# RMS norm rows by one product with ones and a logarithm-exponential pair, and the third norm's steps written among the output projection's blocks

## The chip, the cores and the metric

The kernel runs on one core of a Trainium2 chip. The metric is the device time of one execution in microseconds (us), and the median of three runs stands for a kernel. Engines are named as the profile names them: PE is the matrix engine, DVE the vector engine, ACT the scalar engine (activation functions and copies), POOL the GpSimd engine, SP the engine that issues most transfers.

## The reference, cut to what matters

One layer of a diffusion trunk in fp32: 1024 latent tokens and 256 context tokens of width 1024. Every sublayer starts with an RMS norm modulated by columns made from the condition vector.

```python
def rms_norm(x, w):                       # EPS = 1e-6, mean over the 1024 features
    y = xf * lax.rsqrt(jnp.mean(xf * xf, axis=-1, keepdims=True) + EPS)
    return y * w
def modulate(h, shift, scale):
    return h * (1.0 + scale[:, None, :]) + shift[:, None, :]
def swiglu(h, w1, w3, w2):                # width 2816
    return (jax.nn.silu(h @ w1) * (h @ w3)) @ w2
# x += gate * 0.5 * swiglu(modulate(rms_norm(x)))            (FFN1)
# x += gate * mix(modulate(rms_norm(x)))   retention and gated-linear-attention heads,
#                                          input projection w_in, output projection w_out
# x += gate * 0.5 * swiglu(modulate(rms_norm(x)))            (FFN2)
# final rms_norm of the latent tokens
```

The gated heads need logarithms of a sigmoid of their gate, which the kernel makes with absolute value, exponential and logarithm.

## The kernel before

**Layout.** Activations lie transposed in the on-chip memory: features on the 128 partitions, 8 blocks of 128 features (`KD`), tokens along the row. Tokens come in three groups `tg`: 0 and 1 are 512 latent tokens each, 2 is the 256 context tokens. A norm's factor is one number a token, so along the row, and must stand on all 128 partitions before it can multiply a block.

**Products.** An fp32 product is three products of rounded halves. A weight tile `raw` arrives by DMA, ACT writes its rounded high half `whi`, DVE the rest `wlo` = `raw` - `whi`; activations likewise have `hh` and `hl`. PE then adds hh by whi, hl by whi and hh by wlo. So no block of weights can be used on PE before both ACT and DVE have passed over it. The FFN products use a scheme of seven products in place of eight.

**Order of the work.** Two stretches (from the start to FFN1's first products, and from the end of FFN1 to the end of the mixing, about 845 to 1444 us of the profile) are recorded first by the class `Recorder`: its `run` plans them with a table of costs, picks at each moment the operation with the smallest key on each engine, and pins that order, so each engine runs its instructions strictly in that order. The rest is ordered by the framework's scheduler, with priorities (`low`). The planner keeps the activation function set that it takes to be loaded in `table`; where a planned operation is of another kind it counts 1.3 us and, for "exp", puts a `preload_act_table_set("natural_log_exp_and_others")` (a set with both logarithm and exponential) ahead of it. The compiler adds a load of its own ahead of each activation whose function is not in the set that it finds loaded. These are the rows ACT_TABLE_LOAD.

**The norm.** `squares` adds up the squares of the 8 blocks (ACT squares, DVE adds) in `nacc`, still 128 partial sums a token. `rstd_col` lets PE multiply each 128 tokens of `nacc` by a column of ones (four 128x1 products), after which the sums stand one token to a partition; DVE scales them and adds EPS (`nr`), POOL raises them to the power -0.5. `rows_diag` makes a diagonal matrix `ndiag` for each 128 tokens (DVE, in some places ACT), and `rstd_rows` multiplies it by a matrix of ones on PE, which spreads the factors over all partitions. ACT copies that to `nrb`. `norm_k` then makes, for each block, `nt` = x * scale * nrb (DVE), `hh` (ACT, with the shift) and `hl` (DVE). The context's first norm (`ctx_norm`) already works by products with ones, a logarithm and an exponential.

There are nine such norms: two latent ones at the start, `tg` 2, 1 and 0 at FFN1's end (steps `norm2(tg, i)` of a plan by slots, the last of them recorded), two ahead of FFN2 (`norm_t`, called by `mixed_out` after each latent group's output projection), and two parts of the final norm, in the last steps of the down products, whose outputs `no` are scaled from `nrb` in the PSUM.

`mixed_out` runs over the latent groups, in each over 8 output blocks m: load and split the weights of the block (`load_halves`), 24 products (`proj`), and an add into x on DVE. After FFN1, `hidden` and the down products of FFN2 follow; `t_split` and `first2` make the first sums that FFN2's scheme needs.

Of the kernel before, what the change touches and what calls it, by code (L numbers as in the profile page):

```python
# [165 lines left out]
class Recorder:  # L166
# [145 lines left out]
    def run(self):  # L312
# [6 lines left out]
        kind = True  # L319
        cand, table, pipe, order = [o for o in self.ops if not o.left], None, lead, []  # L320
        while cand:
# [63 lines left out]
            o.made = made[-1]  # L385
            if o.name == "matmul" and any(r.slot and r.slot.tag == "ndiag" for r in o.roots):
                self.diags.append(made[0])
# [18 lines left out]
class Trunk:  # L406
    def __init__(self, ctx, tc, I, out, outt):
        self.tc, self.nc, self.I, self.out, self.outt = tc, tc.nc, I, out, outt
        self.ctx = ctx
        self.uid = 0  # L410
        self.ns, self.ndg = NS, 2
# [32 lines left out]
    def consts(self):  # L444
# [7 lines left out]
        self.mhalf = self.tile(cp, [P, 8], F32, "mhalf")  # L452
        nc.vector.memset(self.mhalf, -0.5)
        self.mods = self.tile(cp, [P, 112], F32, "mod")
# [111 lines left out]

    def rstd_col(self, acc, n, pool, low=None, w=1, ps=None):
        nc = self.nc
        nb = n // P
        ps = self.psN() if ps is None else ps  # L570
        for b in range(nb):
            with self.low(low):
                nc.tensor.matmul(ps[:, b * w:(b + 1) * w], acc[:, b * P:(b + 1) * P], self.ones[:, 0:w], start=True, stop=True)
        r = self.tile(pool, [P, 8], F32, "nr", 2)
        self.pow_half(r[:, :nb], ps[:, 0:nb * w:w], 1.0 / D)
        return r

    def rows_diag(self, r, b, pool, eng=None):
        dg = self.tile(pool, [P, P], F32, "ndiag", self.ndg)
        if eng:  # L580
            eng.activation(dg, self.ident, AF.Copy, scale=r[:, b:b + 1])
        else:
            self.nc.vector.tensor_scalar(out=dg, in0=self.ident, scalar1=r[:, b:b + 1], scalar2=None, op0=ALU.mult)
        return dg

    def rstd_rows(self, r, n, pool, low=None, dg=None, pr=None, eng=None):
        nc = self.nc
        pr = self.psN() if pr is None else pr
        for b in range(n // P):
            d = dg[b] if dg else self.rows_diag(r, b, pool, eng)  # L590
            with self.low(low):
                nc.tensor.matmul(pr[:, b * P:(b + 1) * P], self.ones, d, start=True, stop=True)
        return pr[:, :n]

    def rstd(self, xk, n, pool, low=None):
        r = self.rstd_col(self.squares(xk, n, pool), n, pool, low)
        pr = self.rstd_rows(r, n, pool, low)
        rb = self.scr(pool, "nrb")
        self.nc.scalar.copy(rb[:, :n], pr)
        return rb[:, :n]  # L600

# [24 lines left out]
    def norm_t(self, tg, a, b, pool, tp):  # L626
        tt = self.nc.vector.tensor_tensor
        rb = self.rstd(self.x[tg], TGS[tg][1], pool)
        if tg == 0:
            self.tr = [self.tile(tp, [P, 512], F32, f"t3h{k}") for k in range(4)]  # L630
            for k in range(KD):
                self.norm_k(tg, k, a, b, rb, pool, self.tr[k] if k < 4 else None)
            return
        self.t1r = [self.tile(tp, [P, 512], F32, f"t2{n}{k}") for k in range(2) for n in "hl"]
# [509 lines left out]
    def ctx_norm(self, cx, n1, get):  # L1144
        nc = self.nc
        eps = self.tile(n1, [P, 1], F32, "eps")
        nc.vector.memset(eps, EPS)
        pr, acc = self.psB(), None
# [12 lines left out]
        rb = self.scr(n1, "nacc", 1)[:, :CTX]  # L1161
        nc.scalar.activation(rb, pr[:, :CTX], AF.Ln, bias=eps, scale=1.0 / D)
        nc.scalar.activation(rb, rb, AF.Exp, scale=-0.5)
        return rb
# [127 lines left out]
    def lat_open(self, xp, n1, swap):  # L1292
# [4 lines left out]
        for tg in LATTG:  # L1297
            x = self.x[tg]
            acc = self.squares(x, 512, n1, "", range(4))
            yield  # L1300
            r = self.rstd_col(self.squares(x, 512, n1, "", range(4, KD), acc), 512, n1)
            pr = self.rstd_rows(r, 512, n1, eng=self.nc.scalar)
            rb = self.scr(n1, "nrb", 1)
            self.nc.scalar.copy(rb, pr)
            yield
# [671 lines left out]
    def final(self, tg, o, n, pool, ks):  # L1977
# [17 lines left out]
    def run(self):  # L1995
# [30 lines left out]
        self.mod = [self.mods[:, :72], self.mods[:, 72:]]  # L2026
        self.ndg = 2
        nn, tp = Pool(), Pool()
# [44 lines left out]
        n2 = opn("n2", "right")  # L2073
        self.ndg = 4
        self.x = {tg: [self.tile(xp, [P, 512], F32, f"x{tg}{k}") for k in range(KD)] for tg in LATTG}
# [11 lines left out]
        def norm_step(tg, i, a, b):  # L2087
            with self.low(NLOW if tg == 1 and i in (1, 2) else None):
                norm_part(tg, i, a, b)

        def norm_part(tg, i, a, b):
# [4 lines left out]
            elif i == 1:  # L2096
                nrm[tg] = self.rstd_col(nrm[tg], n, n2)
            elif i == 2:
                pr = self.rstd_rows(nrm[tg], n, n2)
                nrm[tg] = self.scr(n2, "nrb")[:, :n]  # L2100
                self.nc.scalar.copy(nrm[tg], pr)
            else:
                self.norm_k(tg, i - 3, a, b, nrm[tg], n2)

# [18 lines left out]
        def norm1(k):  # L2123
            self.h[1].append(self.hslot(f"1{k}"))
            norm2(1, 3 + k)
# [4 lines left out]
        plan[p2 + 6].append(lambda: norm2(2, 2))  # L2130
# [49 lines left out]
        for i, _ in enumerate(self.ctx_k(f1)):  # L2180
            if i in (3, 5):
                norm2(0, i // 2)
        self.ctx_v(f1)
        for k in range(KD):
            norm2(0, 3 + k)
        spill(0)
        rec.event(lambda: (cls("n2"), cls("hc"), cls("xp")), (n2, hc, xp))
        self.ndg = 2
        self.cp2, mx = Pool(), Pool()
# [17 lines left out]
        self.psN, self.ndg = self.psB, 4  # L2207
        self.mixed_out(self.mcol(5), lambda tg: (self.alloc_h((tg,), self.hp),
                                                 self.norm_t(tg, self.mcol(7), self.mcol(6), n3, tp)))
        rec.run()  # L2210
        self.ndg = 2
        real = lambda ts: [t.root.real for t in ts]
# [19 lines left out]
        raw = self.first2(tp, rec.diags[-4])  # L2232
        late = (None for _ in self.mods_half(f2, (8,)))
# [19 lines left out]
NR = 6  # L2253
HELD = 6
EMODS = ((5, (0,)), (2, (0, 1)), (4, (0, 1)), (3, (0, 1)), (7, (0,)), (6, (0,)))
# [120 lines left out]
```

## Time and profile before

| what | value |
|---|---|
| runs | 2072.51, 2073.89, 2075.93 us; median 2073.89 |
| profiled execution | 2074.48 us, span of the trace 2072.7 us |
| granted PE clock | 0.997 of full speed |
| instructions | 33751 |
| PE | busy 2054.0 us (99% of the span) |
| DVE | busy 1519.2 us (73%) |
| ACT | busy 984.0 us (47%) |
| POOL | busy 68.1 us (3%) |
| rows ACT_TABLE_LOAD | 22, each 1283 ns |

A row of the profile gives the line, the engine, the operation, the tile written and the tiles read with their sizes, the busy time and the mean time of one; after the last bar or in brackets stands the idle time of the engine just before, and what ended it. L147 is the line at which the recorder issues everything that it recorded. Matmuls are pipelined: the time between the starts of two is what one costs, its row's length is longer.

### The profile page before, as it was taken

The page shows a single profiled execution, that of the slowest core. Times are in us where ns is not written, and L with a number is a line of the kernel's source. Part 1 is how long each engine was busy: PE and PEld are TensorE (multiplying, and loading weights), DVE is VectorE, ACT ScalarE, POOL GpSimd, SP SyncE. Part 2 cuts the span into 40 slices and gives each one's busy share as a digit, 9 for nine tenths or more (in the row PEclk, how much of TensorE's full clock was granted, in tenths as well). Part 3 has the DMA queues.
Part 4 walks back from the last instruction along what each step waited for, and adds up shares of the span by engine and source line. Part 5 has one row for each costly group of instructions (what it writes and reads, how often), then busy time and mean ns, then how long its engine had stood idle before and what let it go on. Part 6 is the DMA issues. An engine that isn't in the chain of part 4 may idle for free.

```text
span 2072.7 us, 33751 instructions
## 1 busy us (share of the span) xinstructions
PE 2054.0 (99%) x12137; PEld 1745.8 (84%) x12137; DVE 1519.2 (73%) x2775; ACT 984.0 (47%) x1819; POOL 68.1 (3%) x107
## 2 busy tenths in 40 slices
PE   9999999999999999999999999999999999999998
PEld 8998888888888888898788988888888888888888
DVE  5788789899876778755677478768766666765676
ACT  4765433433445445556475255444434344344553
POOL 0000000000000000001021001000000000010000
PEclk9999999999999999999999999999999999999999
DMA  9765566677788766564233233242344444477674
GB/s 353 229 206 166 166 206 201 223 236 240 255 311 290 248 231 192 177 198 138 68 112 91 90 94 100 86 164 84 107 163 147 146 160 158 153 242 230 219 234 152
DMA packets 210088, 376.39 MB, mean 182 GB/s; under 512 B 23936, under 2 KB 44160, under 8 KB 209792
## 3 DMA queue, kind: packets, MB, share of 16 engines
q1 hardware_dynamic: 209632, 374.10, 55.4%
q8 instruction: 95, 1.56, 0.3%
q14 instruction: 73, 0.60, 0.1%
q10 hardware_dynamic: 288, 0.13, 0.0%
HBM read 292.74 MB, written 73.01 MB: 176 GB/s over the span
## 4 chain that ended last, share of the span: by engine, by line
PE 96%; DVE 2%; DMA 1%; ACT 0%; issue 0%; SPq 0%; POOLq 0%; DVEq 0%; ACTq 0%
PE psa L147 24%; PE psa L440 11%; PE psa L442 11%; PE psa L441 11%; PE psb L147 10%; PE psb L440 9%; PE psb L442 9%; PE psb L441 9%; DMA ada<-in_adaN 1%; DVE nt L147 0%; DVE hl L147 0%; DVE nt L606 0%; PE psb L1957 0%; DMA rs<-rq 0%; DVE S L147 0%
## 5 line engine op out<-in xcount | busy, mean ns | idle before, releaser
L435 ACT ACTIVATE whi<-raw 128x512 fp32r<-128x512 f32 x385 | 243.1, 632 | 516.4 <-issue 181.6
L436 DVE TENSOR_TENSOR wlo<-raw,whi 128x512 fp32r<-128x512 f32 x385 | 264.8, 688 | 159.5 <-ACT whi L435 153.3
L440 PE MATMUL psa<-hh,whi 128*128 128x512 f32 x676 | 263.3, 390 | 0.6 <-ACT s L734 0.6
L442 PE MATMUL psa<-hh,wlo 128*128 128x512 f32 x676 | 263.1, 389 | 0.0
L441 PE MATMUL psa<-hl,whi 128*128 128x512 f32 x676 | 263.0, 389 | 0.0
L147 PE MATMUL psa<-hh,whi 128*128 128x512 f32 (+1 forms) x664 | 234.3, 354 | 0.7 <-ACT whi L147 0.4
L147 PE MATMUL psa<-hh,wlo 128*128 128x512 f32 (+1 forms) x664 | 233.2, 352 | 0.1
L147 PE MATMUL psa<-hl,whi 128*128 128x512 f32 (+1 forms) x664 | 232.9, 351 | 0.0
L440 PE MATMUL psb<-hh,whi 128*128 128x512 f32 x584 | 227.6, 390 | 0.0
L442 PE MATMUL psb<-hh,wlo 128*128 128x512 f32 x584 | 227.2, 389 | 0.0
L441 PE MATMUL psb<-hl,whi 128*128 128x512 f32 x584 | 227.2, 389 | 0.0
L147 DVE TENSOR_TENSOR wlo<-raw,whi 128x512 fp32r<-128x512 f32 (+1 forms) x217 | 139.6, 662 | 102.0 <-ACT whi L147 92.5
L147 ACT ACTIVATE whi<-raw 128x512 fp32r<-128x512 f32 (+1 forms) x217 | 130.3, 609 | 151.6 <-PE psa L147 112.1
L440 PEld LDWEIGHTS psa<-hh,whi 128*128 128x128 f32 x676 | 126.9, 188 | 27.3 <-ACT s L734 1.0
L442 PEld LDWEIGHTS psa<-hh,wlo 128*128 128x128 f32 x676 | 126.9, 188 | 26.3
L441 PEld LDWEIGHTS psa<-hl,whi 128*128 128x128 f32 x676 | 126.9, 188 | 26.3
L147 PEld LDWEIGHTS psa<-hh,whi 128*128 128x128 f32 x664 | 126.2, 190 | 17.5 <-issue 1.0
L147 PEld LDWEIGHTS psa<-hh,wlo 128*128 128x128 f32 x664 | 126.0, 190 | 15.1 <-DVE wlo L147 0.3
L147 PEld LDWEIGHTS psa<-hl,whi 128*128 128x128 f32 x664 | 125.8, 190 | 14.8 <-DVE wlo L147 0.4
L442 PEld LDWEIGHTS psb<-hh,wlo 128*128 128x128 f32 x584 | 109.6, 188 | 22.7
L440 PEld LDWEIGHTS psb<-hh,whi 128*128 128x128 f32 x584 | 109.7, 188 | 22.6
L441 PEld LDWEIGHTS psb<-hl,whi 128*128 128x128 f32 x584 | 109.6, 188 | 22.6
(491 smaller groups left out, 4219.0 us busy)
## 6 DMA issues: line engine op xcount, KB each, us to landing
raw<-in_w SPq DMA_DIRECT2D x316, 256.0 KB, 3.3
gd<-s SPq DMA_DIRECT2D x154, 256.0 KB, 2.9
raw<-gd SPq DMA_DIRECT2D x102, 256.0 KB, 2.9
ada<-in_adaT SPq DMA_DIRECT2D x48, 512.0 KB, 4.1
s<-in_w SPq DMA_DIRECT2D x66, 256.0 KB, 4.5
hh<-in_w SPq DMA_DIRECT2D x55, 256.0 KB, 4.5
sd<-s SPq DMA_DIRECT2D x44, 256.0 KB, 2.7
raw<-sd SPq DMA_DIRECT2D x44, 256.0 KB, 3.4
```

Source lines behind the costliest of these rows:

```text
L147: self.rec.add(self.eng, lambda: f(*map(get, a), **{x: get(v) for x, v in k.items()}), outs, ins, name, a, k)
L435: nc.scalar.activation(hi, src, AF.Copy)
L436: (eng or nc.vector).tensor_tensor(out=lo, in0=src, in1=hi.bitcast(F32), op=ALU.subtract)
L440: mm(ps, wa[0], xa[0], start=start, stop=False, skip_group_check=more)
L441: mm(ps, wa[0], xa[1], start=False, stop=False, skip_group_check=more)
L442: return mm(ps, wa[1], xa[0], start=False, stop=stop, skip_group_check=more)
```

## The change

Between `squares` and `norm_k`, `rstd_rows` now has one PE product of `nacc` with the 128x128 ones over the whole row (512 or 256 tokens), which adds up the partitions and spreads the sum in one, and `root`, two ACT instructions: the logarithm of sum / 1024 + EPS, read from PSUM, and the exponential of -0.5 times that, which is left in `nrb`. The column products, `nr`, the power on POOL, the diagonals and their products, and the copy are gone. EPS stands in a column of `mhalf`. Outside the recorded stretches `root` puts a preload of the set with both functions ahead, under a manual schedule; inside, the recorder's planner now begins with `table` = "exp" where it began with None. The steps of the norm plan have one index less and stand in earlier slots. `mixed_out` takes `norm_t` as a generator: while group 1's blocks are projected, one or two of group 0's norm steps are issued after each block. `HELD`, the number of first sums of FFN2 held ahead, goes from 6 to 4.

```diff
-        cand, table, pipe, order = [o for o in self.ops if not o.left], None, lead, []
+        cand, table, pipe, order = [o for o in self.ops if not o.left], "exp", lead, []
...
-    def rstd_col(self, acc, n, pool, low=None, w=1, ps=None):
...
-        for b in range(nb):
-            with self.low(low):
-                nc.tensor.matmul(ps[:, b * w:(b + 1) * w], acc[:, b * P:(b + 1) * P], self.ones[:, 0:w], start=True, stop=True)
-        r = self.tile(pool, [P, 8], F32, "nr", 2)
-        self.pow_half(r[:, :nb], ps[:, 0:nb * w:w], 1.0 / D)
...
-            self.nc.vector.tensor_scalar(out=dg, in0=self.ident, scalar1=r[:, b:b + 1], scalar2=None, op0=ALU.mult)
...
-                nc.tensor.matmul(pr[:, b * P:(b + 1) * P], self.ones, d, start=True, stop=True)
...
-        self.nc.scalar.copy(rb[:, :n], pr)
...
+    def rstd_rows(self, acc, n, pool, low=None, tag="nrb", bufs=2):
+        pr = self.psN()[:, :n]
+        with self.low(low):
+            self.nc.tensor.matmul(pr, self.ones, acc[:, :n], start=True, stop=True)
+        rb = self.tile(pool, [P, 512], F32, tag, bufs)[:, :n]
+        self.root(rb, pr)
+        return rb
+
+    def root(self, rb, pr):
+        recorded = isinstance(self.nc, Bundle)
+        with nullcontext() if recorded else self.tc.manual_schedule(engines={mybir.EngineType.Activation}):
+            if not recorded:
+                self.nc.scalar.preload_act_table_set("natural_log_exp_and_others")
+            self.nc.scalar.activation(rb, pr, AF.Ln, bias=self.eps, scale=1.0 / D)
+            self.nc.scalar.activation(rb, rb, AF.Exp, scale=-0.5)
...
     def norm_t(self, tg, a, b, pool, tp):
+        self.alloc_h((tg,), self.hp)
         rb = self.rstd(self.x[tg], TGS[tg][1], pool)
+        yield
         if tg == 0:
...
                 self.norm_k(tg, k, a, b, rb, pool, self.tr[k] if k < 4 else None)
+                yield
...
     def mixed_out(self, gcol, after):
+        work = iter(())
...
-            after(tg)
+                for _ in range(1 + m % 2):
+                    next(work, None)
+            for _ in work:
+                pass
+            work = after(tg)
...
-        r = self.rstd_col(acc, n, pool)
+        pr = self.rstd_rows(acc, n, pool, tag="nrb" if tg else "nrbm", bufs=1)
         yield
-        pr = self.rstd_rows(r, n, pool)
...
-        plan[p4 + 4].append(lambda: norm2(1, 2))
...
-            plan[p2 + 7 + k // 2].append(lambda k=k: norm2(2, 3 + k))
-            plan[p4 + 6 + k // 2].append(lambda k=k: norm1(k))
+            plan[p2 + 7 + k // 2].append(lambda k=k: norm2(2, 2 + k))
+            plan[p4 + 3 + k // 2].append(lambda k=k: norm1(k))
...
-HELD = 6
+HELD = 4
```

Counted over the whole program: PE loses 32 128x1 column products and 32 128x128 diagonal products for nine products with ones (seven of 512 tokens, two of 256); DVE loses 33, POOL nine and ACT fifteen instructions (eight diagonals, seven copies); ACT gains nine logarithms, nine exponentials and 29 loads (51 rows ACT_TABLE_LOAD for 22).

**DVE behind FFN1's last products (846 us in the profile).** The first recorded mixing products follow there on PE. `nacc`, `wlo` and `nt`, `hl` are as above; `nrb` is group 1's. Before:

```order
L147 TENSOR_TENSOR wlo_8956<-raw_8895,whi_8913 128x512
L583 TENSOR_SCALAR ndiag_8676<-ident_82,nr_8600 128x128
L147 TENSOR_TENSOR nacc_1960_8822<-nacc_1960_8822,nsq_8946 128x512
L583 TENSOR_SCALAR ndiag_8679<-ident_82,nr_8600 128x128
L583 TENSOR_SCALAR ndiag_8682<-ident_82,nr_8600 128x128
L147 TENSOR_TENSOR wlo_8968<-raw_8897,whi_8921 128x512
L583 TENSOR_SCALAR ndiag_8685<-ident_82,nr_8600 128x128
L147 TENSOR_TENSOR nacc_1960_8822<-nacc_1960_8822,nsq_8960 128x512
L147 TENSOR_TENSOR wlo_8987<-raw_8899,whi_8938 128x512
L147 TENSOR_TENSOR nacc_1960_8822<-nacc_1960_8822,nsq_8971 128x512
L147 TENSOR_TENSOR wlo_9006<-raw_8901,whi_8950 128x512
L606 SCALAR_TENSOR_TENSOR nt_8740<-x_1204_6043,mod_88,nrb_8688 128x512
```

Now, from the same place:

```order
L147 TENSOR_TENSOR nacc_1943_8778<-nacc_1943_8778,nsq_8873 128x512
L147 TENSOR_TENSOR wlo_8900<-raw_8839,whi_8857 128x512
L147 TENSOR_TENSOR nacc_1943_8778<-nacc_1943_8778,nsq_8890 128x512
L592 SCALAR_TENSOR_TENSOR nt_8612<-x_1191_6007,mod_89,nrb_8555 128x512
L592 SCALAR_TENSOR_TENSOR nt_8618<-x_1192_6008,mod_89,nrb_8555 128x512
L147 TENSOR_TENSOR wlo_8912<-raw_8841,whi_8865 128x512
L604 SCALAR_TENSOR_TENSOR hl_1890_8611<-nt_8612,mod_89,hh_1889_8610 128x512
L604 SCALAR_TENSOR_TENSOR hl_1893_8617<-nt_8618,mod_89,hh_1892_8616 128x512
L592 SCALAR_TENSOR_TENSOR nt_8648<-x_1193_6009,mod_89,nrb_8555 128x512
L592 SCALAR_TENSOR_TENSOR nt_8654<-x_1194_6010,mod_89,nrb_8555 128x512
L147 TENSOR_TENSOR nacc_1943_8778<-nacc_1943_8778,nsq_8904 128x512
L604 SCALAR_TENSOR_TENSOR hl_1902_8647<-nt_8648,mod_89,hh_1901_8646 128x512
```

The diagonals are gone. Before, four of the `wlo` of the mixing's weights stand ahead of the first `nt`; now one does, and the next three (of `raw_8841`, `raw_8843` and `raw_8845`) stand behind two, ten and sixteen of the norm's `nt` and `hl`.

**ACT at the gates of the context's heads (946 us).** `t` are tiles of gate values, read from PSUM, then an exponential and a logarithm in place; `sc` and `L` are exponentials; `whi` and `s` as above, and the two copies into `t` feed PE. Before:

```order
L147 ACTIVATE t_2246_10139<-psb_10127,cols_80 128x512
L147 ACTIVATE t_2246_10139<-t_2246_10139 128x512 x2
L147 ACTIVATE t_2250_10162<-psb_10129,cols_80 128x512
L147 ACTIVATE t_2250_10162<-t_2250_10162 128x512 x2
L147 COPY t_2256_10178<-psb_9822 128x256
L147 ACTIVATE sc_10131<-sc_10131 128x512
L147 ACTIVATE whi_10191<-raw_9971 128x512
L147 COPY t_2263_10198<-psb_10166 128x256
L147 ACTIVATE whi_10204<-raw_9991 128x512
L147 COPY s_2259_10220<-psb_10208 128x256
L147 ACTIVATE L_10173<-L_10173 128x508
```

Now:

```order
L147 ACTIVATE t_2217_10082<-psb_10062,cols_80 128x512
L147 ACTIVATE t_2217_10082<-t_2217_10082 128x512
L147 ACT_TABLE_LOAD
L147 ACTIVATE t_2217_10082<-t_2217_10082 128x512
L147 ACTIVATE t_2221_10101<-psb_10064,cols_80 128x512
L147 ACT_TABLE_LOAD
L147 ACTIVATE t_2221_10101<-t_2221_10101 128x512
L147 ACT_TABLE_LOAD
L147 ACTIVATE t_2221_10101<-t_2221_10101 128x512
L147 COPY s_2230_10117<-psb_10070 128x256
L147 ACT_TABLE_LOAD
L147 ACTIVATE sc_10066<-sc_10066 128x512
```

Four loads stand where none stood; between here and the last gate, some eighty instructions on, there are twelve.

**ACT at the start.** `nacc` and `nsq` are the squares of the context's first norm, then its logarithm (read from `psb`) and exponential. Before:

```order
L2015 ACT_TABLE_LOAD
L147 ACTIVATE cexp_121<-cols_80 128x16
L147 ACTIVATE nacc_139<-cx_9_117 128x512
L147 ACTIVATE nsq_143<-cx_9_117 128x512
L147 ACTIVATE nsq_148<-cx_10_129 128x512
L147 ACTIVATE nsq_153<-cx_10_129 128x512
L147 ACTIVATE nacc_168<-psb_157,eps_119 128x256
L147 ACTIVATE nacc_168<-nacc_168 128x256
L147 COPY csum_186<-psb_164 128x128
```

Now:

```order
L2004 ACT_TABLE_LOAD
L147 ACTIVATE cexp_122<-cols_80 128x16
L581 ACT_TABLE_LOAD
L147 ACTIVATE nacc_137<-cx_9_118 128x512
L147 ACTIVATE nsq_141<-cx_9_118 128x512
L147 ACTIVATE nsq_146<-cx_10_130 128x512
L581 ACT_TABLE_LOAD
L147 ACTIVATE nsq_151<-cx_10_130 128x512
L581 ACT_TABLE_LOAD
L147 ACTIVATE nacc_166<-psb_155,mhalf_86 128x256
L581 ACT_TABLE_LOAD
L147 ACTIVATE nacc_166<-nacc_166 128x256
```

The first load was there; the four others, of line 581, stand ahead of and between the context norm's own steps.

More of the change, by code (lines that the diff above doesn't have):

```diff
@@ L385, in run @@
             o.made = made[-1]
-            if o.name == "matmul" and any(r.slot and r.slot.tag == "ndiag" for r in o.roots):
+            if o.name == "matmul" and any(r.slot and r.slot.tag == "nacc" for r in o.roots):
                 self.diags.append(made[0])
@@ L410, in __init__ @@
         self.uid = 0
-        self.ns, self.ndg = NS, 2
+        self.ns = NS
         self.cp = ctx.enter_context(tc.tile_pool(name="cp", bufs=1))
@@ L452, in consts @@
         self.mhalf = self.tile(cp, [P, 8], F32, "mhalf")
-        nc.vector.memset(self.mhalf, -0.5)
+        self.eps = self.mhalf[:, 7:8]
+        nc.vector.memset(self.mhalf[:, :7], -0.5)
+        nc.vector.memset(self.eps, EPS)
         self.mods = self.tile(cp, [P, 112], F32, "mod")
@@ L565, in squares @@
         return acc
-    def rstd_col(self, acc, n, pool, low=None, w=1, ps=None):
-        nc = self.nc
-        nb = n // P
-        ps = self.psN() if ps is None else ps
-        for b in range(nb):
-            with self.low(low):
-                nc.tensor.matmul(ps[:, b * w:(b + 1) * w], acc[:, b * P:(b + 1) * P], self.ones[:, 0:w], start=True, stop=True)
-        r = self.tile(pool, [P, 8], F32, "nr", 2)
-        self.pow_half(r[:, :nb], ps[:, 0:nb * w:w], 1.0 / D)
[L576 to L598, printed above, removed]
-        self.nc.scalar.copy(rb[:, :n], pr)
-        return rb[:, :n]
+    def rstd_rows(self, acc, n, pool, low=None, tag="nrb", bufs=2):
[5 more added lines that the diff above has]
+        return rb
@@ new lines, in root, with rstd @@
+    def root(self, rb, pr):
[5 more added lines that the diff above has]
+            self.nc.scalar.activation(rb, rb, AF.Exp, scale=-0.5)
+    def rstd(self, xk, n, pool):
+        return self.rstd_rows(self.squares(xk, n, pool), n, pool)
@@ L1145, in ctx_norm @@
         nc = self.nc
-        eps = self.tile(n1, [P, 1], F32, "eps")
-        nc.vector.memset(eps, EPS)
         pr, acc = self.psB(), None
@@ L1161, in ctx_norm @@
         rb = self.scr(n1, "nacc", 1)[:, :CTX]
-        nc.scalar.activation(rb, pr[:, :CTX], AF.Ln, bias=eps, scale=1.0 / D)
-        nc.scalar.activation(rb, rb, AF.Exp, scale=-0.5)
+        self.root(rb, pr[:, :CTX])
         return rb
@@ L1300, in lat_open @@
             yield
[L1301 to L1304, printed above, removed]
+            rb = self.rstd_rows(self.squares(x, 512, n1, "", range(4, KD), acc), 512, n1, bufs=1)
             yield
@@ L1930, in mixed_out @@
                 nc.vector.scalar_tensor_tensor(out=x, in0=ps, scalar=gcol[:, m:m + 1], in1=x, op0=ALU.mult, op1=ALU.add)
-            after(tg)
+                for _ in range(1 + m % 2):
[3 more added lines that the diff above has]
+            work = after(tg)
+        for _ in work:
+            pass
     def final_diag(self):
@@ L2026, in run @@
         self.mod = [self.mods[:, :72], self.mods[:, 72:]]
-        self.ndg = 2
         nn, tp = Pool(), Pool()
@@ L2073, in run @@
         n2 = opn("n2", "right")
-        self.ndg = 4
         self.x = {tg: [self.tile(xp, [P, 512], F32, f"x{tg}{k}") for k in range(KD)] for tg in LATTG}
@@ L2087, in norm_step @@
         def norm_step(tg, i, a, b):
-            with self.low(NLOW if tg == 1 and i in (1, 2) else None):
+            with self.low(NLOW if tg == 1 and i == 1 else None):
                 norm_part(tg, i, a, b)
@@ L2096, in norm_part @@
             elif i == 1:
[L2097 to L2101, printed above, removed]
+                nrm[tg] = self.rstd_rows(nrm[tg], n, n2)
             else:
-                self.norm_k(tg, i - 3, a, b, nrm[tg], n2)
+                self.norm_k(tg, i - 2, a, b, nrm[tg], n2)
         def first1(k):
@@ L2124, in norm1 @@
             self.h[1].append(self.hslot(f"1{k}"))
-            norm2(1, 3 + k)
+            norm2(1, 2 + k)
         p2, p4 = 5 * NP, 6 * NP
@@ L2129, in run @@
         plan[p2 + 4].append(lambda: norm2(2, 1))
-        plan[p2 + 6].append(lambda: norm2(2, 2))
         for i in range(4):
@@ L2180, in run @@
         for i, _ in enumerate(self.ctx_k(f1)):
-            if i in (3, 5):
-                norm2(0, i // 2)
+            if i == 5:
+                norm2(0, 1)
         self.ctx_v(f1)
         for k in range(KD):
-            norm2(0, 3 + k)
+            norm2(0, 2 + k)
         spill(0)
         rec.event(lambda: (cls("n2"), cls("hc"), cls("xp")), (n2, hc, xp))
-        self.ndg = 2
         self.cp2, mx = Pool(), Pool()
@@ L2206, in run @@
                 self.nc.sync.dma_start(self.x[tg][k], self.xd[k * P:(k + 1) * P, o:o + n])
-        self.psN, self.ndg = self.psB, 4
-        self.mixed_out(self.mcol(5), lambda tg: (self.alloc_h((tg,), self.hp),
-                                                 self.norm_t(tg, self.mcol(7), self.mcol(6), n3, tp)))
+        self.psN = self.psB
+        self.mixed_out(self.mcol(5), lambda tg: self.norm_t(tg, self.mcol(7), self.mcol(6), n3, tp))
         rec.run()
-        self.ndg = 2
         real = lambda ts: [t.root.real for t in ts]
@@ L2231, in run @@
                 self.t_split(tp, i, k, raw[k])
-        raw = self.first2(tp, rec.diags[-4])
+        raw = self.first2(tp, rec.diags[-1])
         late = (None for _ in self.mods_half(f2, (8,)))
```

## The prediction

> **What bounds the kernel now.** I read the page's busy times and chain first, then the list of what PE waits for, then the chain of waits and the timelines at the places that the change touches.
>
> ```profile
> PE 2054.0 (99%) x12137; PEld 1745.8 (84%) x12137; DVE 1519.2 (73%) x2775; ACT 984.0 (47%) x1819; POOL 68.1 (3%) x107
> ACT  4765433433445445556475255444434344344553
> PE 96%; DVE 2%; DMA 1%; ACT 0%; issue 0%; SPq 0%; POOLq 0%; DVEq 0%; ACTq 0%
> ```
>
> PE is busy in 2054.0 of 2072.7 us and is the chain. So the change can pay in two ways only: fewer products, or shorter waits of PE. It can cost where PE, which runs its list in order, comes to a product whose input is late. The waits (engine, tile and line, what it waited for: us in total, times, longest) are few:
>
> ```profile
> PE psb L147 <- issue: 2.5, 1, 2.5
> PE psb L592 <- DVE ndiag L583: 2.3, 1, 2.3
> PE psb L147 <- DVE wlo L147: 2.1, 2, 1.7
> PE psb L147 <- DMA ada<-in_adaN: 1.7, 2, 0.9
> ```
>
> Two of them lie in the norm of group 1 at FFN1's end, which the change rebuilds. The chain there (start, length, what):
>
> ```profile
> 844.88 0.80 PE psb L573 x8
> 845.70 0.16 DVE nr L1628
> ...
> 847.64 0.29 DVE ndiag L583
> ...
> 848.47 3.66 PE psb L147 x18
> 852.12 0.22 PE psb L592 x2
> ...
> 853.07 0.59 ACT nrb L2101
> 853.69 1.15 DVE nt L606 x2
> ...
> 865.59 8.13 PE psb L147 x54
> 873.72 6.32 PE psa L147 x48
> ```
>
> The eight records of four column products take 0.80 us; then PE stands for 2.3 us behind nr, POOL's power and the first diagonal. The row 848.47 has 18 products of 256 columns at 0.203 us each. The timeline of PE gives the usual distance, and the windows the granted clock:
>
> ```profile
> 853.11 0.28 PE L147 MATMUL psb<-hh,whi 128*128 128x256 f32 x1
> 853.23 0.28 PE L147 MATMUL psb<-hl,whi 128*128 128x256 f32 x1
> ...
> 0.00:19.00 19.00, 15.34 (x141) 12.94 (x145) 8.11 (x23) 9.08 (x18) 0.39 (x6) 1.00 0.92 331
> 840.00:880.00 40.00, 35.62 (x248) 34.31 (x247) 32.24 (x61) 22.06 (x44) 2.32 (x2) 0.91 0.49 152
> 946.00:1000.00 54.00, 53.87 (x314) 44.51 (x313) 36.40 (x87) 38.89 (x92) 6.62 (x14) 1.00 0.51 148
> 1380.00:1446.00 66.00, 65.40 (x299) 53.81 (x298) 53.49 (x89) 32.86 (x54) 1.68 (x2) 1.00 0.23 72
> ```
>
> (Columns after the window's length: busy PE, PEld, DVE, ACT, POOL, then the granted clock, the DMA share and GB/s.) A product's start is 0.12 us after the last at full clock, so the 18 at 0.203 lost (0.203 - 0.12) x 18 = 1.5 us to a lower clock: the window 840 to 880 was granted 0.91, every other of these 1.00. Missing clock of 0.09 x 40 = 3.6 us at half speed is two such losses of 1.5 to 1.8 us, one behind each stall. So a stall of 2 us or more costs about 1.6 us again.
>
> **The change, part by part.**
>
> *Products.* The new product's price is read from the context's first norm, which already works so (two products of 256 columns are four records):
>
> ```profile
> 7.71 1.13 PE L147 MATMUL psb<-nacc,ones 128*128 128x256 f32 x4
> 8.68 1.03 PE L147 MATMUL psb<-nsq,ones 128*128 128x256 f32 x4
> ```
>
> Start to start 8.68 - 7.71 = 0.97 us for 512 columns. Removed are the columns, 0.80 us, and four diagonal products of 0.22 us each (row 852.12), 0.88: 1.68 - 0.97 = 0.7, and 0.8 with the changes of shape between them, for which I have no row of their own; I take 0.75. The two norms of 256 tokens save half. Together 7 x 0.75 + 2 x 0.37 = 6.0 us, of which two norms, 1.5 us, lie in the place reckoned next. Elsewhere: **-4.5 us**. All of it is on the path, since PE is.
>
> *ACT's loads.* ACT gets 29 more of these, each 1.28 us:
>
> ```profile
> L147 ACT ACT_TABLE_LOAD x11 | 14.1, 1283 | 0.2
> ...
> 896.27 0.59 ACT L147 COPY s<-psa 128x512 f32<-128x512 f32 x1 [0.19 <-PE psa L147]
> 896.88 1.28 ACT L383 ACT_TABLE_LOAD   x1
> 898.17 0.21 ACT L147 ACTIVATE cdec<-mod 128x8 f32<-128x8 f32 x1
> ```
>
> The next activation starts as the load ends, so I price one at 1.28. The Trainium skill's "ScalarE: Activation LUTs" (What ACT_TABLE_LOAD costs) puts every switch at about 2.66 us, 1.28 for the load and 1.38 for a drain; this row shows the first part and no drain. Most loads fall where ACT has room (the page's slices: four to six tenths busy) and PE has weights in hand, at 0 us: the two at the context rows' norm near 800, the pairs at the first latent norms, the four at the end. Three places are dearer.
>
> *FFN1's end, 845 to 874.* PE's product with ones runs at 844.9 to 845.8. ACT and DVE rows that price what follows:
>
> ```profile
> 845.24 1.13 ACT L147 ACTIVATE whi<-raw 128x512 fp32r<-128x512 f32 x2
> ...
> 850.23 0.68 DVE L147 TENSOR_TENSOR wlo<-raw,whi 128x512 fp32r<-128x512 f32 x1
> ...
> 853.69 1.42 DVE L606 SCALAR_TENSOR_TENSOR nt<-x,mod,nrb 128x512 f32<-128x512 f32 x2 [1.57 <-ACT nrb L2101]
> ...
> 855.63 1.41 DVE L618 SCALAR_TENSOR_TENSOR hl<-nt,mod,hh 128x512 fp32r<-128x512 f32 x2
> ```
>
> After its `whi` at 845.8, ACT has load, logarithm, `whi`, load, exponential: 1.28 + 0.6 + 0.5 + 1.28 + 0.6 = 4.3, so the row is ready at 850.1, 3.5 us before the 853.66 of before. But DVE, in order, now stands at `nt` until 850.1 with only one of the mixing's `wlo` done behind the last adds. The `wlo` of raw_8841 comes after two `nt` (1.33 + 0.6: 852.1), that of raw_8843 after ten norm steps and an add (858.7), that of raw_8845 after six more and an add (863.9). PE has 28 products that need none of these: 28 x 0.12 = 3.4, from 845.8 to 849.2. So it waits 2.9; then some fifteen products (at half clock, 0.21, to 855.3), a wait of 3.4 to 858.7, eight more to 860, a wait of 3.9 to 863.9. These are 10.2 us of waiting against 2.3 + 2.1 = 4.4 before, at two to three slow stretches against two. Less the 1.5 of the products: 10.2 - 4.4 - 1.5 = 4.3; **+4.3 us**. Ends: -8 if DVE's order delays no weight (the 4.4 and half of two clock losses gone, and 1.5 of products, and some 0.5 in PE's list), +6 with one clock loss more.
>
> *The gates, 946 to 1000.* Here one load served before; now the set alternates and twelve stand in ACT's list, 12 x 1.28 = 15.4 us. The window shows ACT busy 38.89 of 54, so 15.1 us of room, with products of PE between that wait for ACT:
>
> ```profile
> 946.20 0.69 ACT L147 ACTIVATE t<-psb,cols 128x512 f32<-128x512 f32 x1
> 946.92 1.30 ACT L147 ACTIVATE t<-t 128x512 f32<-128x512 f32 x2
> ...
> 950.02 0.35 ACT L147 COPY t<-psb 128x256 f32<-128x256 f32 x1
> 950.28 0.63 ACT L147 ACTIVATE sc<-sc 128x512 f32<-128x512 f32 x1
> ...
> 951.62 1.89 PE L147 MATMUL psb<-t,t 128*128 128x256 f32 x8
> ```
>
> The copy into t at 950.02 now follows four loads (5.1), a copy of 0.27 and `sc` (0.53): 955.9. PE's products of t with t stood at 951.62; in the new list about 1.3 us of other products more stand ahead of them, so 952.9. The copies' results were used 1.6 us after the first began; 955.9 + 1.0 to 1.6 = 957.2, a wait of 4.0 to 4.6; I take 4.0. It puts PE back too, which eases the later ones: by the same count the third pair of t is 1 to 2 us late (1.0). One loss of clock, 1.6. **+6.6 us**; ends 0 (PE's products of the input projection could cover all, if its place in the list lies later than I count) and +15 (all loads on the path).
>
> *The start.* Four loads stand in the context norm's chain:
>
> ```profile
> 6.30 1.39 ACT L147 ACTIVATE nsq<-cx 128x512 f32<-128x512 f32 x2 [0.67 <-DMA cx<-in_ctxP]
> 9.75 0.47 ACT L147 ACTIVATE nacc<-psb,eps 128x256 f32<-128x256 f32 x1 [2.05 <-PE psb L147]
> ```
>
> Loads take 5.1 us, idle time of ACT there is 0.67 + 2.05: 2.4 to 2.9 us later. PE then waits less for the DMA of ada (1.7 above) and had other gaps, 15.34 busy of 19: 2.7 - 1.7 = **+1.0 us**; ends 0 and 2.9.
>
> *The third norm and what else moves.* It begins earlier, among group 1's projection. PE is busy 65.40 of 66 there, so the most to win is 0.6; DVE, 53.49 of 66, has the same work in another order. **-0.4 us**, ends -0.6 and +6 (a rival). Ordering of the recorded stretch in between changes too; PE is at 1.00 and waits nowhere over 0.4 there but for a piece of 2.5 named "issue": 0, +-2. The 33 DVE, nine POOL and fifteen ACT instructions that go were off the path but for the 2.3 us counted.
>
> **Sum:** -4.5 + 4.3 + 6.6 + 1.0 - 0.4 = +7.0. On the profiled execution, 2074.48 us (1.8 outside its span), 2081.5; that run stands 0.6 above the median of 2073.89, so 2080.9. My counts of stalls err high more easily than low, since PE's list has products that I take to be blocked: I say **2080**.
>
> **Rivals.**
>
> *The weights are not late (faster).* At FFN1's end everything turns on whether the `wlo` of raw_8841 to raw_8845 are ready when PE comes to them, from 849.2 on. If the row came by 847.5, or PE's list had 10 us of products free of them, the waits of 4.4 and both clock losses of 3.2 would be gone with 6.0 of products, -13.6; with 0 to 7 left at the gates: 2060 to 2069. For it: the chain's link from 845.8 to 853.7 is what the change shortens. Against: DVE's list as shown. 0.20.
>
> *One of the two places is covered.* Either the gates (2080 - 6.6 = 2073.4) or FFN1's end at no gain or loss (2075.7): 2071 to 2077. For it: PE is granted 1.00 and waits for nothing between 946 and 1000 today, so slack exists that no row shows. 0.18.
>
> *ACT becomes the bound at the gates.* Its room of 15.1 us is less than the 15.4 added. If the room lies in the wrong places, 5 to 10 us more go to PE: 2085 to 2090. 0.10.
>
> *The interleaved norm starves the output projection.* Each block's two `wlo` (0.6 each) can stand behind one or two norm steps of about 3 us on DVE; eight blocks by 0.6: +5, 2084 to 2087. DVE's 12.5 us of room speaks against. 0.05.
>
> *Each load drains ACT.* If a load held ACT for 1.38 us more, twelve would be 16.6 us past the room at the gates: 2090 to 2097. The row at 898.17 shows none. 0.03. That is what the Trainium skill's figure above comes to.
>
> **How the numbers follow.** The forecast, both places late, has 0.44 (2076 to 2086). About 0.2%, 4 us, is what a measurement of this kernel can tell from no change: faster is under 2069.7, slower over 2078.0. Slower: 0.38 of the forecast, 0.10, 0.05 and 0.03, 0.56. Same: 0.06 of the forecast and 0.14 of the second rival, 0.20. Faster: 0.20 and 0.04, 0.24. The range leaves out a tenth at each end: half of the first rival below, the drain and the last of the ACT bound above: 2066 to 2089. The likeliest case's own range is 2076 to 2086.
>
> **What would show it.** Right: 51 loads of 1.28 us; PE waiting for `wlo` around 849, 856 and 860, two or three times for 2.5 to 4 us, with a granted clock under 0.91 in 840 to 880; a wait of about 4 us for t near 953; PE's busy time less clock losses down by some 6 us; nothing new from 1380 to 1446. Wrong: no wait over 2 us in 845 to 874 (then the first rival), none at the gates, or a same-set load at the start shorter than 1.28.

## The result, and the profile after

The changed kernel takes 2085.22 us (median of four runs, 2083.79 to 2088.64) against 2074.91 us for the kernel before in the same comparison. The ratio is 1.0053, 95% interval 1.0036 to 1.0071: slower, by about 10 us. The profiled execution has a span of 2083.7 us, 11.0 more than before.

The page's busy times and chain:

```profile
PE 2054.9 (99%) x12027; PEld 1739.5 (83%) x12027; DVE 1513.2 (73%) x2742; ACT 1023.3 (49%) x1851; POOL 59.6 (3%) x98
PE 83%; issue 11%; DVE 2%; ACT 2%; DMA 1%; POOL 0%; SPq 0%; DVEq 0%; POOLq 0%; ACTq 0%
```

PE still bounds. It has 110 records less (55 products of two records each), yet its busy time is 0.9 us more; more of its work fell into stretches of half clock, as the windows below show. ACT is 39.3 us busier: 29 loads at 1.28 are 37.2 of that. What PE waited for (us in total, times, longest):

```profile
PE psb L147 <- DVE wlo L147: 10.6, 3, 4.6
PE psb L147 <- ACT s L147: 2.7, 1, 2.7
...
PE psb L147 <- ACT csum L147: 1.8, 2, 1.5
PE psa L440 <- ACT s L723: 1.4, 1, 1.4
```

The windows that were shown of before (busy PE, PEld, DVE, ACT, POOL, then the granted clock):

```profile
0.00:19.00 19.00, 15.86 (x125) 13.40 (x125) 5.83 (x17) 12.99 (x20) 0.39 (x6) 0.86 0.92 333
840.00:880.00 40.00, 29.39 (x189) 26.85 (x188) 27.38 (x45) 25.48 (x44) 0.00 (x0) 0.83 0.34 106
946.00:1000.00 54.00, 50.19 (x217) 39.68 (x215) 29.25 (x68) 44.91 (x83) 4.99 (x14) 0.94 0.45 127
1380.00:1446.00 66.00, 66.00 (x289) 53.93 (x289) 46.63 (x72) 32.56 (x51) 0.00 (x0) 1.00 0.29 91
```

The first three lost clock (0.86, 0.83, 0.94 for 1.00, 0.91, 1.00), and two of them lost PE's time as well; the last one, with the interleaved norm, won 0.6. The slow clock at the start reaches past the first window, and the kernel before has a piece of it too, just behind that window (first line before, then two lines of the changed kernel):

```profile
19.00:22.40 3.40, 3.40 (x38) 2.38 (x33) 1.19 (x3) 1.33 (x3) 0.00 (x0) 0.50 1.04 403
12.00:26.00 14.00, 12.44 (x104) 9.86 (x105) 7.38 (x16) 7.03 (x16) 0.00 (x0) 0.63 1.04 403
853.50:867.00 13.50, 6.21 (x28) 5.62 (x27) 11.45 (x18) 4.37 (x7) 0.00 (x0) 0.50 0.30 90
```

The last line shows that a low clock is not a loss of the same size: at FFN1's end half clock was granted for 13.5 us, but PE was busy in only 6.21 of them and waited in the rest.

The four loads of line 581 at the start are the preloads that `root` writes ahead of four norms of 800 to 2061 us. They stand at 4.3 to 11.1 us instead, and at each of those four norms the compiler put two loads of its own, one ahead of the logarithm and one ahead of the exponential:

```profile
4.33 1.28 ACT L581 ACT_TABLE_LOAD   x1
```

Where the 11 us went is read from operations that stand in both traces, by the start of the same one in each:

| up to | operation | later than before, us | the stretch alone |
|---|---|---|---|
| 68 us | PE product of hh with s | +2.2 | start +2.2 |
| 783 | PE product in FFN1's down products | +0.2 | two latent norms -2.0 |
| 844 | DVE's last add into x of FFN1's first group | -0.3 | context rows' norm -0.5 |
| 945 | PE product ahead of the gates | +4.6 | FFN1's end +4.9 |
| 1032 | PE product of vt with sc | +13.4 | gates +8.7 |
| 1328 | PE product of qk with qk | +13.6 | +0.3 |
| 1442 | PE product of hl with t3l | +11.4 | third norm -2.2 |
| 1465 | the same, after FFN2's first Silu | +12.2 | +0.8 |
| 2065 | last column products | +11.1 | tail -1.2 |

FFN1's end in the timelines of ACT, DVE and PE:

```profile
845.58 1.28 ACT L582 ACT_TABLE_LOAD   x1
846.87 0.69 ACT L582 ACTIVATE nrb<-psb,mhalf 128x512 f32<-128x512 f32 x1
...
848.10 1.28 ACT L583 ACT_TABLE_LOAD   x1
849.39 0.63 ACT L583 ACTIVATE nrb<-nrb 128x512 f32<-128x512 f32 x1
...
850.05 1.42 DVE L592 SCALAR_TENSOR_TENSOR nt<-x,mod,nrb 128x512 f32<-128x512 f32 x2 [2.87 <-ACT nrb L583]
851.38 0.68 DVE L147 TENSOR_TENSOR wlo<-raw,whi 128x512 fp32r<-128x512 f32 x1
...
857.89 0.68 DVE L147 TENSOR_TENSOR wlo<-raw,whi 128x512 fp32r<-128x512 f32 x1
...
863.07 1.88 DVE L147 TENSOR_TENSOR wlo<-raw,whi 128x512 fp32r<-128x512 f32 x3
...
852.12 0.39 PE L147 MATMUL psb<-hh,wlo 128*128 128x256 f32 x1 [3.32 <-DVE wlo L147]
858.62 0.58 PE L147 MATMUL psb<-hh,wlo 128*128 128x256 f32 x1 [4.61 <-DVE wlo L147]
863.80 0.58 PE L147 MATMUL psb<-hh,wlo 128*128 128x256 f32 x1 [2.68 <-DVE wlo L147]
```

The row of factors is there at 850.0, 3.6 us earlier than before. DVE had stood 2.87 us for it with weights behind it in its queue, and each `wlo` that then ends (852.06, 858.57, 863.7) releases PE within 0.1 us. The gates:

```profile
952.51 1.28 ACT L147 ACT_TABLE_LOAD   x1
953.80 0.63 ACT L147 ACTIVATE t<-t 128x512 f32<-128x512 f32 x1
...
958.80 0.35 ACT L147 COPY s<-psb 128x256 f32<-128x256 f32 x1
959.17 1.28 ACT L147 ACT_TABLE_LOAD   x1
...
961.00 0.35 ACT L147 COPY t<-psb 128x256 f32<-128x256 f32 x1
...
959.21 0.58 PE L147 MATMUL psb<-p89Tc,wg 128*128 128x256 f32 x1 [2.70 <-ACT s L147]
961.41 3.79 PE L147 MATMUL psb<-t,t 128*128 128x256 f32 x8 [0.34 <-ACT t L147]
```

PE stops first at a product whose PSUM bank the copy of s at 958.80 has to empty, behind three loads; the products of t with t then run at half clock, 3.79 us for 1.89 before.

### The profile page after: what moved, and what is told of

The parts are those of the page before. It is cut to its first block, busy times and chain, and to the rows that moved or that the text cites. A ratio compares the mean times of both kernels' runs of the same rounds, so it can differ in the third digit from the quotient of the medians.

```text
span 2083.7 us, 33514 instructions
## 1 busy us (share of the span) xinstructions
PE 2054.9 (99%) x12027; PEld 1739.5 (83%) x12027; DVE 1513.2 (73%) x2742; ACT 1023.3 (49%) x1851; POOL 59.6 (3%) x98
## 4 chain that ended last, share of the span: by engine, by line
PE 83%; issue 11%; DVE 2%; ACT 2%; DMA 1%; POOL 0%; SPq 0%; DVEq 0%; POOLq 0%; ACTq 0%
PE psa L147 23%; PE psb L147 10%; PE psa L440 9%; PE psa L441 9%; PE psa L442 9%; PE psb L440 8%; PE psb L441 8%; PE psb L442 8%; ACT L147 0%; DVE wlo L147 0%; DVE hl L147 0%; DVE nt L147 0%; DMA hl<-in_w 0%; DVE nt L592 0%; POOL wd L1928 0%
```

## The experiments

All kernels but one come from the changed one; PE's order stays the same in them, or differs in some ten rows where that is said. Each ratio is to the kernel before on the same chip, whose median was 2073.85 or 2075.38 us, so kernels are compared by ratios. What a stretch gains or loses is read as in the table above.

**The loads at the start alone.** In `root`:

```diff
-            if not recorded:
-                self.nc.scalar.preload_act_table_set("natural_log_exp_and_others")
```

> The changed kernel without the preload that root puts ahead outside the recorded stretches; the four loads at the start are gone (47 loads for 51), the order of PE and DVE is the same, and the first norm works with the set that the program loads at its start. Theory (loads on ACT delay the first norm by 2.2 us): the rows after 25 us come 2.0 to 2.4 us earlier, time 2083.0 (from 2085.2), ratio to before about 1.0042. Rival (the wait there is for the ada transfers and another cause is late next): under 0.7 us gained, 2084.5 or more.

Measured: 2081.48 us, ratio 1.0033 (1.0020 to 1.0047). At 68 us it is 2.0 earlier than before, 4.2 earlier than the changed kernel.

```profile
0.00:19.00 19.00, 16.30 (x152) 13.75 (x152) 7.89 (x23) 9.23 (x18) 0.39 (x6) 1.00 0.92 338
```

The granted clock is 1.00 again. The gain is twice what was expected, since the four loads had cost clock as well as time: from 12 to 26 us the changed kernel was granted 0.63, this one 1.00. Of the 2.0 that it is ahead of the kernel before, most is that kernel's own slow piece at 19.0 to 22.4. Between 844 and 945 it loses 4.9 us, as the changed kernel does, and 6.7 from there to 1032 (8.7).

**The loads at the gates alone.** In the recorder's `run`:

```diff
-        cand, table, pipe, order = [o for o in self.ops if not o.left], "exp", lead, []
+        cand, table, pipe, order = [o for o in self.ops if not o.left], None, lead, []
```

> The changed kernel with the planner's table None at the start of a recorded stretch, as before, so that one load of the set with both functions stands ahead of group 0's norm at FFN1's end and none at the context's gates (38 loads for 51; nine rows of PE's order differ). Theory (the twelve loads make PE wait at 946 to 1000, and what runs late there also costs the 3.6 us that are lost between 1000 and 1022): 5.0 + 3.6 gained and 1 at FFN1's end, 2076 to 2078, ratio 1.001 to 1.002; no wait of PE for s or t over 0.6 between 946 and 1000. Rival (the new order of the recorded stretch costs the 3.6): 2079.5 to 2081. Rival (the order costs both): 2084 or more.

Measured: 2077.71 us, ratio 1.0013 (1.0004 to 1.0022). From 945 to 1032 us it loses 0.6 against before, where the changed kernel loses 8.7.

```profile
946.00:1000.00 54.00, 54.00 (x307) 44.38 (x307) 34.67 (x80) 36.30 (x82) 6.64 (x14) 1.00 0.50 142
```

PE has no idle time left there and full clock; the theory holds in time and place, and the new order of the stretch is not the cause.

**The same loads in the kernel before.** The opposite edit, in the kernel before:

```diff
-        cand, table, pipe, order = [o for o in self.ops if not o.left], None, lead, []
+        cand, table, pipe, order = [o for o in self.ops if not o.left], "exp", lead, []
```

> The kernel before, with one word changed: the recorder's planner begins with the table "exp", so that the one load ahead of the gates is not made and the compiler puts loads among the gates instead (32 loads for 22); the norms are as before. Theory (the loads at the gates cost PE some 8 us, whatever the norms do): 2080 to 2083, ratio 1.003 to 1.0045, PE waiting for s or t between 946 and 1000. Rival (the loss at the gates needs the changed kernel's other delays): 2073 to 2076.

Measured: 2083.86 us, ratio 1.0039 (1.0027 to 1.0051); +8.6 us from 945 to 1032. The waits:

```profile
PE psb L147 <- ACT s L147: 2.7, 1, 2.7
PE psb L592 <- DVE ndiag L583: 2.3, 1, 2.3
PE psb L147 <- DVE wlo L147: 2.3, 3, 1.7
...
PE psb L147 <- ACT t L147: 1.9, 2, 1.1
```

With the old norms, diagonals and all, the loads alone make the same wait of 2.7 for s and the same loss. This is the largest single part of the change's cost, and it comes from one word.

**DVE's order at FFN1's end alone.** Group 1's norm steps get a lower priority, so five `wlo` stand ahead of the first `nt`:

```diff
-            with self.low(NLOW if tg == 1 and i == 1 else None):
+            with self.low((NLOW if i == 1 else 300 if i > 1 else None) if tg == 1 else None):
```

> The changed kernel with group 1's norm steps at FFN1's end at a lower priority, so that five of the mixing's wlo stand on DVE ahead of the first nt; all 51 loads stay, PE's order is the same. Theory (the 10.6 us that PE waits there come from DVE's order, not from the loads): the three waits for wlo fall to 2 us or less together and the slow clock with them: 10 to 14 us gained, 2071 to 2076, ratio 0.999 to 1.0005. Rival (the row of factors is late because of the two loads ahead of it, and whatever waits for it is late in any order): less than 4 us gained, 2081 or more, with a wait of PE for hh or hl of group 1 instead.

Measured: 2080.79 us, ratio 1.0028 (1.0018 to 1.0038). Both expectations missed. From 844 to 945 us it loses 1.0 for 4.9, but not the 10 to 14 us forecast:

```profile
PE psa L147 <- DVE wlo L147: 4.7, 1, 4.7
...
PE psb L147 <- DVE wlo L147: 2.5, 3, 1.7
```

The three old waits fell from 10.6 to 2.5 as the theory said, and one of 4.7 opened behind them: the context's v weights (into psa) come after the norm steps that were put back. The lateness moved down DVE's queue: of 10.6 us of waiting only 3.4 went. The loads still reach DVE here by another way, a square that ACT writes behind two of them:

```profile
850.56 0.69 DVE L147 TENSOR_TENSOR nacc<-nacc,nsq 128x512 f32<-128x512 f32 x1 [2.79 <-ACT nsq L147]
```

**The loads alone, at all three places.** The changed kernel with one load, tied to its place, for the context rows' norm (`pin` is true there alone, `lastsq` is that norm's last square); the set then stays until the gates are done, so that the planner's "exp" is true:

```diff
-            if not recorded:
-                self.nc.scalar.preload_act_table_set("natural_log_exp_and_others")
+            p = None
+            if not recorded and self.pin:
+                p = self.nc.scalar.preload_act_table_set("natural_log_exp_and_others")
+                self.tc.add_manual_dep(p.ins, self.lastsq.ins.name, SCHED, reason="order")
...
+            if p:
+                self.tc.add_manual_dep(ln.ins, p.ins.name, SCHED, reason="order")
```

> The changed kernel with one load of the set with both functions, tied behind the squares of the context rows' norm, in place of the repeated ones (30 loads for 51); DVE's order at FFN1's end as in the changed kernel, with the norm ahead of the weights. It parts what the loads and what DVE's order cost at FFN1's end. Theory A (DVE's order costs by itself): PE still waits for three wlo, 8 us or more together, and the time is 2068 to 2071. Theory B (the loads make the norm late there, and without them the norm is through before PE needs the weights): waits under 5 us, 2064.6 as with the weights first, within 1.5.

Measured: 2070.86 us, ratio 0.9981 (0.9973 to 0.9990). Theory A: PE still waits 8.0 us for three `wlo`, longest 4.8:

```profile
PE psb L147 <- DVE wlo L147: 8.0, 3, 4.8
```

From 844 to 945 it loses 1.4 us, 3.5 less than with the loads. The first of the three waits fell (0.52 for 3.32); the others did not (4.81 and 2.67 for 4.61 and 2.68).

**Both together,** the last two diffs in one kernel.

> The changed kernel with both: group 1's norm steps at lower priority, and one load of the set with both functions, tied behind the squares of the context rows' norm at FFN1's end, in place of the repeated preloads (30 loads for 51: none at the start, none at FFN1's end after that one, none at the gates). Theory (loads at three places and DVE's order at one are the whole loss, and the nine products give 6 us): 2085.2 - 2.2 - 8.6 - 12 = 2062 to 2066, ratio 0.994 to 0.996, faster than before. Rival (the recorded stretch's new order costs 3 to 4 of it): 2066 to 2070. Rival (the loads cost nothing by themselves): 2071 to 2076, as with the weights first alone.

Measured: 2064.62 us, ratio 0.9950 (0.9936 to 0.9963), as expected: faster than both kernels. At FFN1's end:

```profile
PE psa L147 <- DVE wlo L147: 3.1, 1, 3.1
...
840.00:880.00 40.00, 36.88 (x260) 35.21 (x259) 39.08 (x65) 30.35 (x63) 1.52 (x3) 0.91 0.64 202
```

DVE is now busy 39.08 of 40 us, so what is left of the wait looks like DVE's work rather than its order; no run tests that. From 844 to 945 it gains 3.7 us.

**The interleaving alone.** In `mixed_out` (about ten rows of PE's order differ):

```diff
-                for _ in range(1 + m % 2):
-                    next(work, None)
-            for _ in work:
-                pass
-            work = after(tg)
+            for _ in after(tg):
+                pass
```

> The changed kernel with group 0's third norm written behind its projection in one piece, as before, not among group 1's blocks. Theory (the interleaving keeps PE from waiting at 1380 to 1446 and is worth 0.5 to 1): 2085.5 to 2086.5. Rival (it puts norm steps ahead of the projection's weights on DVE and costs): 2082 to 2084.5.

Measured: 2088.21 us, ratio 1.0061 (1.0048 to 1.0075); the interval overlaps the changed kernel's. The trace decides the sign: between 1328 and 1442 it gains 0.1 where the interleaved one gains 2.2, and PE has a wait that the other lacks:

```profile
PE psa L147 <- DVE wlo L147: 1.8, 1, 1.8
```

So the interleaving is worth about 2 us here, more than expected; the rival falls. The change of `HELD` from 6 to 4 stands in both and was not run apart.

**The Silu's load.** Both together as above, and in the recorder, behind the last operation of kind "exp":

```diff
             made = [call() for call in o.calls]
+            if self.silu and o is self.lastexp:
+                made.append(self.nc.scalar.preload_act_table_set("silu_and_others"))
```

> One load and the weights first, as in one_set_weights, and the load of the set with the Silu placed behind the third norm's last exponential, where ACT has room, in place of just ahead of FFN2's first Silu. Theory (PE's wait of 1.4 for that Silu's output holds 0.8 to 1.3 of load): the wait falls to 0.6 or less, 2063.2 to 2064. Rival (the wait is for the product ahead of the Silu, not for the load): no change, 2064.6.

Measured: 2062.63 us, ratio 0.9941 (0.9929 to 0.9953), the fastest. The interval overlaps the one without this edit, so the runs alone don't show it. The traces do. In the changed kernel the load stands right ahead of the Silu that PE waits for:

```profile
1455.11 1.28 ACT L723 ACT_TABLE_LOAD   x1
1456.41 0.60 ACT L723 ACTIVATE s<-psa 128x512 f32<-128x512 f32 x1
...
1457.06 0.50 PE L440 MATMUL psa<-hh,whi 128*128 128x512 f32 x1 [1.43 <-ACT s L723]
```

With the load moved, `s` follows at once and PE has no wait there; from 1442 to 1465 us the kernel gains 0.5 against before, where the other kernels with the new norms lose 0.8.

## Why the prediction was right, and where its terms were off

It forecast slower, at 2080 (2066 to 2089); 2085 came out, above the forecast and inside its range and its likeliest case's (2076 to 2086). Against the kernel before the trace has +11.0 for the +7.0 of the sum; most of the 4.0 that it missed lies at the gates (2.1) and at the start (1.2).

**FFN1's end: right in place, mechanism and size.** Said: factors at 850.1, `wlo` at 852.1, 858.7 and 863.9, waits of 2.9, 3.4 and 3.9, together 10.2, +4.3. Found: 850.0, 852.06, 858.57, 863.7, waits of 3.3, 4.6 and 2.7, together 10.6, +4.9. Counting the in-order queue of DVE by row times was enough, and counting no more clock loss than before did no harm, because PE waited in more than half of the slow stretch. The runs add what the count could not: the loads hold 3.5 us of this loss and DVE's order 3.9, each by itself, and the order alone only pushes the wait on.

**The gates: right in place, too small.** Said +6.6, found +8.1 (the changed kernel's 8.7 less the 0.6 of the one without these loads). The waits summed to 3.8 us in place of 5.0. What was mis-sized is the clock: one loss of 1.6 was counted, and 0.94 of 54 us is 3.2, two of them. Waits and clock together make 7.0; the other 1.1 is not placed. A wait of about 4 us for `t` near 953 was said to show it; the wait that came is 2.7 for `s` at 959.2, and those for `t` are 0.5 and less.

**The start: too small.** Said +1.0, found +2.2, and 4.2 between the changed kernel and the one without these loads. The step "PE then waits less for the DMA" held: the waits for ada, 1.7 in all, are gone, and those for csum are 1.5 longer. The term that was missing is the clock, 0.63 from 12 to 26 us, which the sum put at nothing. The +2.2 even flatters the change, since the kernel before spent 3.4 us at half clock there as well, without any of these loads.

**The products: right, a little low.** Said 1.5 for the two latent norms, 0.4 for the context rows' and 1.1 for the tail's two; found 2.0, 0.5 and 1.2.

**The third norm: two errors that nearly cancel.** Said -0.4, with "the most to win is 0.6", beside 1.5 for its two products; found -2.2 and then +0.8 from the load ahead of FFN2's Silu, which was counted among those at no cost. Without the interleaving, about 2 of the 2.2 would have gone: the gain of the products would have been lost again in a wait of 1.8 for a weight. That the place comes to -1.4 for the -1.9 said is luck.

**The last step was wrong outright.** The sum came to 2080.9 and was lowered to 2080 on the view that counted stalls err high. The waits at the gates did err high, 5.0 for 3.8, but the start and the gates as wholes came out low once their clock is counted, and nothing in the traces supports the 0.9 taken off.

**The rivals.** The opposite one, weights not late, at 2060 to 2069, is what the kernel does once the loads and DVE's order are both mended (2064.6). It turned on the right point, the weights behind the norm on DVE, but that point alone was not enough: the order alone stays slower than before (1.0028), the loads alone come to 0.9981, and only both give 0.9950. The measured 2085 also lies at the edge of the case that ACT bounds the gates (2085 to 2090) and inside that of the starved output projection (2084 to 2087); the traces speak against both, as ACT was busy 44.91 of 54 us there and PE waited only 3.8, and the interleaving gained time. The drain after each load is refuted: the loads at 952.51 and 845.58 end at 953.79 and 846.86, and the next activations start at 953.80 and 846.87. The figure of 2.66 us for a switch in the Trainium skill's "ScalarE: Activation LUTs" (What ACT_TABLE_LOAD costs) does not hold for these instructions, and its 1283 ns does.

## What to carry to other kernels

An activation function that replaces a chain on other engines brings its table: count the loads in the compiled order, not in the source, because a preload that nothing ties down drifts away from its place, and a planner's belief about the loaded set can be false. Where engines run their queues in order, a result that comes earlier can still cost, if what waits for it stands ahead of the bound engine's next inputs; mend the loads and the queue together, then look where the wait has moved. Count clock losses with stalls of the bound engine: at the start and the gates they were the larger part of what was missed here.

## What the runs showed of the hardware

A stall of PE does not cost the same clock each time. The kernel before and the one with loads at its gates have the same two waits at FFN1's end, 2.3 us for the diagonal and 1.7 for a weight. The one was granted 0.91 of the clock from 840 to 880, the other all of it:

```profile
840.00:880.00 40.00, 35.38 (x273) 34.06 (x272) 35.78 (x67) 25.43 (x53) 3.79 (x5) 1.00 0.54 169
```

By 869 us it had gained 2.5 us on the kernel before, of which a load at 893 took some back (1.2 are left at 945), and at 68 us, ahead of any difference between the two, it was 1.9 earlier. At the start the runs show both luck and cause: the four kernels profiled with the four loads there were all granted 0.63 from 12 to 26 us, and of the six without them four were granted 1.00 and two, the kernel before and the one with the loads mended alone, 0.88. The Trainium skill's "TensorE: Matmul & The Clock Gate" (Part 1: The HAM clock gate) says that activity is judged in windows of 3413 ns that run on their own. The length agrees with these traces, 0.09 of 40 us being two half-speed windows of it. A stall that is cut by a window's edge might then pass unnoticed, but no run here moved a stall within a window, so this reading is not shown. Either way, single profiles differ by 1 to 2.5 us at each of these places without a difference between the kernels that accounts for it, and gains of that size in one trace may be luck.
